# First block's projections taken from x before its norm is known, their products scaled in PSUM; evictions given a higher priority in the recorded order

## The chip, the cores and the metric

The kernel runs on one core of one Trainium2 chip. Its time is the device time of one execution in microseconds (us); lower is better. The kernel before took 1443.79 us, the median of three runs (1440.97, 1443.79, 1444.25). The profile that is read here is of one further execution, which took 1438.14 us; its instructions span 1436.3 us.

## The reference

One layer of a streaming encoder on x of 2048 rows and 1024 columns, float32. The row norm comes first, one input projection feeds three groups of heads, and an output projection with a residual and a second row norm ends it.

```python
hn = rmsnorm(x, norm_g)                       # x * rsqrt(mean(x*x) + EPS) * g
z = jnp.einsum('bsd,de->bse', hn, w_in)       # split into 16 column groups
att = band_chunk_attention(...)               # 6 heads, own 64-row chunk and 8 before it
h_ml = mlstm_chunkwise(...)                   # 6 heads, matrix memory; conv + SiLU on q, k
h_gla = gla_chunkwise(...)                    # 4 heads, per-channel decay from a low-rank gate
y = jnp.concatenate([y_a, y_b, y_c], axis=-1) # each times its own SiLU gate
out = rmsnorm(x + jnp.einsum('bse,ed->bsd', y, w_out), final_g)
```

The row norm multiplies a row of x by one number, and the projection is linear. So the projection of x times g can be taken first and each row's product multiplied by that row's number afterwards: the result is the same up to rounding.

## The kernel before, in words

The rows are cut into four blocks of 512 (`q` = 0 to 3). The projections run block after block; the attention and the output projection follow in a second part, which the change leaves alone.

**One projection.** A projection group fills one PSUM bank `ip` (128 by 512) with 24 matmuls: eight pieces of the contraction, three products each (`x` and `w` are split into a high and a low part in the fp32r format; high by high, high by low, low by high). `proj_g` (L243 to L245) keeps the output columns on the partitions, `proj_t` (L263 to L265) the rows. There are two `ip` banks. TensorE can start the group after next only when both engines that read a bank have read it: that reading is called the eviction (`proj_v`, `silu_tile`, `att_in` and others), done by ScalarE (ACT) and VectorE (DVE). Weights come by DMA into two raw buffers `wraw`, are cast to the high part by ACT (L235) and get their low part from DVE or, for every third one, from GpSimd (POOL) (L236). Five split weights fit at a time.

**The block's norm.** `prep_x` reads the 512 rows of x as they stand (four DMAs), squares and sums them on ACT (L286), takes the power -0.5 on POOL (L288) and puts the 512 numbers on the diagonals of four matrices on DVE (L291). `prep` spreads them over all partitions with one matmul by ones (L298) and a copy (L300), reads the transposed x, `xT`, into four buffers `xraw`, multiplies it by g and the row numbers on DVE (L307) and makes the small gate projection from it (L314). `split_x` makes the high part (ACT, L328) and the low part (DVE or POOL, L329). Only block 0 does this ahead of all projections; blocks 1 to 3 have it done while the block before is projected. `gates` then takes two selections of the gate rows (L336, L343) and runs a chain of logarithms, scans and exponentials on ACT and DVE (L272 to L374).

**The chains.** While a block is projected, three generators put their own matmuls between the projection's: `gla_in` and `gla` (the third head group) and `mlstm` (the second). `gla_in` makes 32 element products per block on POOL (`prd`, L642; `gk`, L639), in groups of four buffers; after each group TensorE sums the four (L648) and so frees the buffers. `gla` needs the blocks `Kt` from POOL (L675) for its matmuls L682.

**What sets the order.** TensorE's order is written by hand: `Flow.piece` adds up the planned time of the projection's matmuls, and a generator's next part is put in when the planned gap after its last part, the second number that it yields, is over. `Flow.need` puts in all that is left of a chain at once. The order on the other engines is made by a scheduler from priorities; `tc.high_priority(offset=AHEAD)` raises the priority of what is issued within it. Each engine runs its own order strictly in turn. At `flow.need("gla_in")`, after the gate projections `proj_gm` of blocks 0, 1 and 2, the rest of `gla_in` is put in with no projection between: this stretch is called the cluster below. After block 3 the chains run out alone: the tail.

## Time and profile before

| | us |
|---|---|
| median of three runs | 1443.79 |
| profiled execution, its own time | 1438.14 |
| its span | 1436.3 |
| TensorE busy in the span | 1325.9 |
| VectorE busy | 791.9 |
| ScalarE busy | 601.7 |
| GpSimd busy | 621.2 |
| first matmul of a block projection | 32.43 |
| last two chains of block 3 run out alone | 981 to 1014 |

The mean granted clock of TensorE was 0.943 of full. A profile line names the line of the kernel, the engine, the operation, and the tiles as output<-inputs; `PE` is TensorE's matmuls, `PEld` its weight loads, `SPq` the queue that issues the DMAs. A wait is put down to the instruction that released it. A busy time of TensorE is not its peak, since matmuls overlap: a group of 24 in a row takes about 5.4 us at the full clock whatever their busy times add up to.

### The profile page before, as it was taken

The page shows a single profiled execution, that of the slowest core. Times are in us where ns is not written, and L with a number is a line of the kernel's source. Part 1 is how long each engine was busy: PE and PEld are TensorE (multiplying, and loading weights), DVE is VectorE, ACT ScalarE, POOL GpSimd, SP SyncE. Part 2 cuts the span into 40 slices and gives each one's busy share as a digit, 9 for nine tenths or more (in the row PEclk, how much of TensorE's full clock was granted, in tenths as well). Part 3 has the DMA queues.
Part 4 walks back from the last instruction along what each step waited for, and adds up shares of the span by engine and source line. Part 5 has one row for each costly group of instructions (what it writes and reads, how often), then busy time and mean ns, then how long its engine had stood idle before and what let it go on. Part 6 is the DMA issues. An engine that isn't in the chain of part 4 may idle for free.

```text
span 1436.3 us, 20063 instructions
## 1 busy us (share of the span) xinstructions
PE 1325.9 (92%) x7044; PEld 1073.8 (75%) x7044; DVE 791.9 (55%) x1886; ACT 601.7 (42%) x1149; POOL 621.2 (43%) x847
## 2 busy tenths in 40 slices
PE   5899989989998998999899899997878999999997
PEld 2688867868886786888678677886766887877876
DVE  7626546762654666264466625646556756656731
ACT  5634312463431246343133524332356555655531
POOL 4215662321665222266533415743246354453442
PEclk7999979999997999999799999998987999999999
DMA  7443214554321455432144533331488464655322
GB/s 248 147 131 100 85 39 123 151 176 128 103 74 39 118 153 178 126 107 73 45 119 126 140 120 104 89 112 49 134 215 257 143 182 128 183 155 156 102 69 87
DMA packets 107206, 180.11 MB, mean 125 GB/s; under 512 B 9824, under 2 KB 54752, under 8 KB 107104
## 3 DMA queue, kind: packets, MB, share of 16 engines
q1 hardware_dynamic: 102496, 170.43, 40.1%
q10 hardware_dynamic: 4608, 8.39, 1.6%
q8 instruction: 56, 0.92, 0.3%
q14 instruction: 46, 0.38, 0.1%
HBM read 143.14 MB, written 35.65 MB: 124 GB/s over the span
## 4 chain that ended last, share of the span: by engine, by line
PE 70%; DVE 10%; DMA 6%; POOL 5%; ACT 4%; issue 4%; SPq 1%; POOLq 0%; DVEq 0%; ACTq 0%
PE ip L243 12%; PE ip L245 12%; PE ip L244 12%; PE s L851 3%; PE ip L975 3%; PE ip L973 3%; PE ip L974 3%; PE ip L263 3%; PE ip L264 3%; PE ip L265 2%; PE tp L915 2%; PE ga L682 2%; DVE pt L865 2%; PE s L554 2%; PE w L932 2%
## 5 line engine op out<-in xcount | busy, mean ns | idle before, releaser
L243 PE MATMUL ip<-x,w 128*128 128x512 f32 x800 | 327.5, 409 | 0.0
L245 PE MATMUL ip<-x,w 128*128 128x512 f32 x800 | 314.0, 393 | 0.0
L244 PE MATMUL ip<-x,w 128*128 128x512 f32 x800 | 314.0, 392 | 0.0
L235 ACT CAST w<-wraw 128x1024 fp32r<-128x1024 f32 x132 | 138.3, 1048 | 264.3 <-PE ip L245 189.9
L236 DVE TENSOR_TENSOR w<-wraw,w 128x1024 fp32r<-128x1024 f32 x88 | 115.3, 1310 | 181.1 <-ACT w L235 180.5
L236 POOL TENSOR_TENSOR w<-wraw,w 128x1024 fp32r<-128x1024 f32 x44 | 106.2, 2413 | 205.6 <-ACT w L235 205.5
L243 PEld LDWEIGHTS ip<-x,w 128*128 128x128 f32 x800 | 151.5, 189 | 43.2 <-issue 13.9
L245 PEld LDWEIGHTS ip<-x,w 128*128 128x128 f32 x800 | 151.3, 189 | 33.2
L244 PEld LDWEIGHTS ip<-x,w 128*128 128x128 f32 x800 | 151.8, 190 | 31.2 <-issue 2.4
L870 POOL TENSOR_SCALAR pt<-pt,sm 128x640 f32<-128x640 f32 (+2 forms) x96 | 70.7, 738 | 150.1 <-DVE sm L869 117.6
L263 PE MATMUL ip<-w,x 128*128 128x512 f32 x256 | 105.2, 411 | 23.1 <-DVE hl L414 21.8
L264 PE MATMUL ip<-w,x 128*128 128x512 f32 x256 | 103.5, 404 | 3.5 <-POOL w L236 2.7
L973 PE MATMUL ip<-wo,y 128*128 128x512 f32 x256 | 106.6, 416 | 0.0
L868 ACT ACTIVATE pt<-pt,sm 128x640 f32<-128x640 f32 (+2 forms) x96 | 73.3, 764 | 71.2 <-DVE sm L865 68.6
L265 PE MATMUL ip<-w,x 128*128 128x512 f32 x256 | 103.0, 402 | 0.0
L975 PE MATMUL ip<-wo,y 128*128 128x512 f32 x256 | 101.2, 395 | 0.3 <-POOL y L881 0.3
L974 PE MATMUL ip<-wo,y 128*128 128x512 f32 x256 | 101.2, 395 | 0.0
L642 POOL TENSOR_TENSOR prd<-gk,zg 128x16 f32<-128x16 f32 (+15 forms) x128 | 75.3, 588 | 59.2 <-PE pw L648 53.0
L921 DVE TENSOR_TENSOR pl<-tp,ph 128x512 fp32r<-128x512 f32 (+2 forms) x126 | 74.6, 599 | 32.4 <-ACT ph L920 31.0
L851 PE MATMUL s<-kk,qq 128*128 128x384 f32 (+1 forms) x360 | 80.9, 335 | 10.2 <-DVE sm L865 8.7
L851 PEld LDWEIGHTS s<-kk,qq 128*128 128x128 f32 x360 | 61.0, 202 | 28.7 <-DVE sm L865 21.9
L263 PEld LDWEIGHTS ip<-w,x 128*128 128x128 f32 x256 | 50.2, 196 | 36.4 <-DVE hl L414 23.5
(244 smaller groups left out, 2447.2 us busy)
## 6 DMA issues: line engine op xcount, KB each, us to landing
wraw<-in_w_f SPq DMA_DIRECT2D x100, 512.0 KB, 3.6
wraw<-in_w_t SPq DMA_DIRECT2D x32, 512.0 KB, 4.0
qq<-q_d SPq DMA_DIRECT2D x48, 256.0 KB, 4.5
kk<-k_d SPq DMA_DIRECT2D x18, 512.0 KB, 6.6
vv<-v_d SPq DMA_DIRECT2D x18, 512.0 KB, 7.5
xraw<-in_x SPq DMA_DIRECT2D x16, 512.0 KB, 5.3
xraw<-in_xT SPq DMA_DIRECT2D x16, 512.0 KB, 7.2
xr<-in_x SPq DMA_DIRECT2D x16, 512.0 KB, 4.0
```

What stands on the lines that cost most here:

```text
L235: nc.scalar.copy(w[:, :, 0, :], rv)
L236: other().tensor_tensor(w[:, :, 1, :], rv, f32(w[:, :, 0, :]), op=ALU.subtract)
L243: nc.tensor.matmul(ps, w[:, k, 0, :], X[k][:, 0, :], start=(k == 0), stop=False)
L244: nc.tensor.matmul(ps, w[:, k, 0, :], X[k][:, 1, :], start=False, stop=False)
L245: nc.tensor.matmul(ps, w[:, k, 1, :], X[k][:, 0, :], start=False, stop=(k == KT - 1))
L263: nc.tensor.matmul(ps, X[k][:, 0, t], w[:, 0, :], start=(k == 0), stop=False)
L264: nc.tensor.matmul(ps, X[k][:, 0, t], w[:, 1, :], start=False, stop=False)
L265: nc.tensor.matmul(ps, X[k][:, 1, t], w[:, 0, :], start=False, stop=(k == KT - 1))
L851: nc.tensor.matmul(sp[:, :cn], qq[:, l, tt * P:(tt + 1) * P], kk[:, ko + c0:ko + c0 + cn], start=(l == 0), stop=(l == 1))
L973: nc.tensor.matmul(ps, Y[k][:, 0, t], wo[k, j][:, 0, :], start=(e == 0), stop=False)
L974: nc.tensor.matmul(ps, Y[k][:, 0, t], wo[k, j][:, 1, :], start=False, stop=False)
L975: nc.tensor.matmul(ps, Y[k][:, 1, t], wo[k, j][:, 0, :], start=False, stop=(e == KT - 1))
```

## The change

Five things are changed.

- **Block 0 starts from raw x.** The rows of x are not read for block 0; `xT` is, at once after the first weight and the vector g. `first_x` makes the high part of x times g on ACT (L277), the low part on DVE (L278), and eight tiles of squares of x, four on ACT and four on POOL. `first_z` projects `gq`; after each of the eight pieces four float32 matmuls (L293) add that piece's squares over the partitions, by a column of ones, into the bank `ss`. From this come the row numbers `rs`, the diagonals `dg`, and, after the group `gk`, the spread numbers `rbs`. `gq` and `gk` are multiplied by them as they are evicted; the gate projection uses weights times g and is multiplied as well.
- **All later products of block 0** are multiplied in their bank before their eviction: DVE L338 in `proj_t` (8 times), DVE L263 in `proj_f` (24 times).
- **Evictions** in `proj_t`, `silu_tile`, `proj_z`, `proj_m` and `att_in` are issued within `tc.high_priority(offset=AHEAD)`.
- **Two planned gaps are shorter:** 6.0 in place of 7.0 before each summing of `gla_in`, 0.5 in place of 4.0 after each chunk of `gla`.
- Calls are moved so that this holds; the other blocks' norms are made as before.

```diff
         def proj_f(name, X):
...
+            if "rbs" in lead:
+                scale_f(out_[0])
             return out_[0]
+        def scale_f(ps):
+            with tc.high_priority(offset=AHEAD):
+                nc.vector.tensor_tensor(ps, ps, lead["rbs"], op=ALU.mult)
+        def first_x():
+            raws, X, sq = [], [], []
+            with tc.high_priority(offset=2 * AHEAD):
+                nc.sync.dma_start(ng, norm_g)
+                w0 = load_w(w_f[_F.index("gq")], KT)
+                for g in range(4):
...
+                    nc.sync.dma_start(raw, xT[:, 2 * g:2 * g + 2, 0:QT])
+            for k in range(KT):
+                src = raws[k // 2][:, k % 2, :]
+                xk = xs.tile([P, 2, QT], FR, name="x")
+                nc.scalar.activation(xk[:, 0, :], src, AF.Copy, scale=ng[:, k:k + 1])
+                nc.vector.scalar_tensor_tensor(xk[:, 1, :], src, ng[:, k:k + 1], f32(xk[:, 0, :]), op0=ALU.mult, op1=ALU.subtract)
+                sq.append(g_tile([P, QT]))
+                if k % 2 == 0:
+                    nc.scalar.activation(sq[k], src, AF.Square)
+                else:
+                    nc.gpsimd.tensor_tensor(sq[k], src, src, op=ALU.mult)
...
+        def first_z(R):
+            raws, X, sq, w0 = first_x()
+            ss = bank("pw")
+            for k, _ in enumerate(proj_g("gq", X, out_, 1, w0)):
+                for tt in range(NC):
+                    nc.tensor.matmul(ss[:, tt:tt + 1], sq[k][:, tt * P:(tt + 1) * P], ones[:, 0:1],
...
+            nc.gpsimd.tensor_tensor(rs, rs, mhalf[:, 0:NC], op=ALU.pow)
...
+            for _ in proj_g("gk", X, out_, KT):
+                pass
+            rb = bank("pw")
+            nc.tensor.matmul(rb, ones, dg.rearrange("p a t -> p (a t)"), start=True, stop=True)
...
+            nc.scalar.copy(rbs, rb)
...
+                nc.vector.scalar_tensor_tensor(z[:, 0, :], out_[0], 32.0 ** -0.5, rbs, op0=ALU.mult, op1=ALU.mult)
+                nc.vector.tensor_tensor(z[:, 1, :], out_[1], rbs, op=ALU.mult)
...
-                evac(tt, ps)
+                with tc.high_priority(offset=AHEAD):
+                    if "rs" in lead:
+                        nc.vector.tensor_scalar(ps, ps, lead["rs"][:, tt:tt + 1], None, op0=ALU.mult)
+                    evac(tt, ps)
...
-                        yield 0.0, 7.0
+                        yield 0.0, 6.0
...
-                    yield 0.25, 4.0
+                    yield 0.25, 0.5
...
-        flow.start("prep", prep(0, R, prep_x(0)))
         load_consts()
-        flow.finish("prep")
-        X = split_x(R["raws"])
+        X, z0 = first_z(R)
```

Three places of the new order matter for what follows. Lines after the change are higher by about 70: L272 becomes L343, L414 becomes L487, L642 becomes L721, L675 becomes L754.

**ScalarE at the start.** Before, with `g<-pw` the copy of the spread row numbers:

```order
L286 ACTIVATE xraw,rs<-xraw 128x1024 x3
L235 CAST w<-wraw 128x2x512 x2
L300 COPY g<-pw 128x512
L328 CAST x<-xraw 128x512 x6
L235 CAST w<-wraw 128x2x512
```

Now, with `dd<-pw` that copy:

```order
L277 ACTIVATE x<-xraw,ng 128x512 x3
L281 ACTIVATE g<-xraw 128x512
L235 CAST w<-wraw 128x8x128
L235 CAST w<-wraw 128x2x512 x4
L308 COPY dd<-pw 128x512
L235 CAST w<-wraw 128x2x512
```

The copy stood behind two casts of the value weights (`128x2x512`) and now stands behind four.

**VectorE in the gate chain of block 1.** `hl<-ip` is the eviction of the first value group's banks; the first bank is free after the second of these. Before:

```order
L356 TENSOR_TENSOR g<-g 6x512
L629 TENSOR_TENSOR qt<-zg,qt 128x256
L633 TENSOR_TENSOR Dt<-Dt,dl 128x2
L414 TENSOR_TENSOR hl<-ip,hl 128x3x64
L629 TENSOR_TENSOR qt<-zg,qt 128x256
L633 TENSOR_TENSOR Dt<-Dt,dl 128x2
L628 TENSOR_TENSOR lc<-lc,zg 128x256 x2
L359 TENSOR_TENSOR g<-g 6x512
L633 TENSOR_TENSOR Dt<-Dt,dl 128x2x2 x2
L414 TENSOR_TENSOR hl<-ip,hl 128x3x64
L361 TENSOR_TENSOR g<-g 6x512
```

Now:

```order
L432 TENSOR_TENSOR g<-g 6x512
L436 TENSOR_TENSOR rows<-g,ml 6x128
L437 TENSOR_TENSOR rows<-g 6x384
L712 TENSOR_TENSOR Dt<-Dt,dl 128x2x2
L434 TENSOR_TENSOR hl_nm<-g,hl_nm 6x512
L712 TENSOR_TENSOR Dt<-Dt,dl 128x2x2
L487 TENSOR_TENSOR hl<-ip,hl 128x3x64
L712 TENSOR_TENSOR Dt<-Dt,dl 128x2x3 x2
L445 TENSOR_TENSOR hl_iw<-rows,hl_iw 6x4
L712 TENSOR_TENSOR Dt<-Dt,dl 128x2x4 x2
L712 TENSOR_TENSOR Dt<-Dt,dl 128x2x5
L487 TENSOR_TENSOR hl<-ip,hl 128x3x64
```

L432, L436, L437 and L434 are the old L361, L365, L366 and L363: they stood behind the two evictions and now stand ahead of them.

**TensorE in block 0's cluster.** Before, the cluster's first rows, from the first sum of the second half (`32x256 x4`) on, with no projection between:

```order
L648 MATMUL pw<-prd,hs_157 32x256 x4
L600 MATMUL mt<-ident,m 128x128 x3
L521 MATMUL s<-hl_nm,sel 128x128 x6
L729 MATMUL gb<-ident,n 128x128 x2
L648 MATMUL pw<-prd,hs_157 32x16x5
L648 MATMUL pw<-prd,hs_157 32x16x6
L648 MATMUL pw<-prd,hs_157 32x16x7
L648 MATMUL pw<-prd,hs_157 32x16x8
L531 MATMUL s<-qk 128x128 x6
L535 MATMUL mt<-ident,qk 128x128 x3
L678 MATMUL gb<-ident,dr 128x128
L679 MATMUL gb<-ident,kd 128x128
```

Now its first rows are:

```order
L727 MATMUL pw<-prd,hs_157 32x16x7
L727 MATMUL pw<-prd,hs_157 32x16x8
L679 MATMUL mt<-ident,m 128x128 x3
L600 MATMUL s<-hl_nm,sel 128x128 x6
L808 MATMUL gb<-ident,n 128x128 x2
L757 MATMUL gb<-ident,dr 128x128
L758 MATMUL gb<-ident,kd 128x128
L761 MATMUL ga<-Qb,Kt 128x64 x7
L727 MATMUL pw<-prd,hs_157 32x16x9
L727 MATMUL pw<-prd,hs_157 32x16x10
L727 MATMUL pw<-prd,hs_157 32x16x11
L727 MATMUL pw<-prd,hs_157 32x16x12
```

The first of the four sums (`32x256 x4`) left the cluster: it stands 36 projection matmuls earlier. The `mlstm` matmuls that stood behind the old L682 (L549, L554, L566) left it too, to behind the next half group of the projection. On POOL the seven `Kt` of this chunk (L754) stand behind the products of the third group of four; on TensorE their user L761 stands ahead of that group's sums.

More of the change, by code (lines that the diff above doesn't have):

```diff
@@ L237, in load_w, with proj_g @@
             return w
-        def proj_g(name, X, out_, per):
-            w = load_w(w_f[_F.index(name)], KT)
+        def proj_g(name, X, out_, per, w=None):
+            w = load_w(w_f[_F.index(name)], KT) if w is None else w
             ps = bank("ip", 2)
@@ L394, in sig_tile @@
             th = ev.tile([P, QT], FP32, name="e")
-            nc.scalar.activation(th, ps, AF.Tanh, scale=0.5)
+            with tc.high_priority(offset=AHEAD):
+                nc.scalar.activation(th, ps, AF.Tanh, scale=0.5)
             return th
@@ L430, in proj_z @@
             z = big.tile([P, 2, QT], FP32, name="zg", bufs=1)
-            nc.scalar.activation(z[:, 0, :], proj_f("gq", X), AF.Copy, scale=32.0 ** -0.5)
-            nc.scalar.copy(z[:, 1, :], proj_f("gk", X))
+            pq = proj_f("gq", X)
+            with tc.high_priority(offset=AHEAD):
+                nc.scalar.activation(z[:, 0, :], pq, AF.Copy, scale=32.0 ** -0.5)
+            pk = proj_f("gk", X)
+            with tc.high_priority(offset=AHEAD):
+                nc.scalar.copy(z[:, 1, :], pk)
             return z
@@ L448, in proj_m @@
                 zb = big.tile([P, 3 + QT], FP32, name="u", bufs=1)
-                nc.scalar.copy(zb[:, 3:], ps)
+                with tc.high_priority(offset=AHEAD):
+                    nc.scalar.copy(zb[:, 3:], ps)
                 if st["zb"] is None:
@@ L481, in att_in @@
             scl = 0.125 if b < 3 else 1.0
-            nc.scalar.activation(hl[:, 0, :], ps, AF.Copy, scale=scl)
-            nc.vector.scalar_tensor_tensor(hl[:, 1, :], ps, scl, f32(hl[:, 0, :]), op0=ALU.mult, op1=ALU.subtract)
+            with tc.high_priority(offset=AHEAD):
+                nc.scalar.activation(hl[:, 0, :], ps, AF.Copy, scale=scl)
+                nc.vector.scalar_tensor_tensor(hl[:, 1, :], ps, scl, f32(hl[:, 0, :]), op0=ALU.mult, op1=ALU.subtract)
             if b < 3:
@@ L757, in trunk_kernel @@
             qk = proj_m(X)
+            if lead:
+                rbs = big.tile([P, 3 + QT], FP32, name="u", bufs=1)[:, 0:QT]
+                nc.vector.tensor_copy(rbs, lead["rbs"])
+                lead["rbs"] = rbs
             M = dict(R)
@@ L765, in trunk_kernel @@
             proj_a(q, X)
+            lead.clear()
             if q + 1 < NQ:
```

33 lines of the change are left out of this document (30 added, 3 removed).

## The prediction

> **What bounds the kernel now.** I read the page's engine rows and its chain first, then TensorE's waits up to 1090 us (the projections and the hand-over to the attention; the change leaves the rest alone), then single stretches.
>
> ```profile
> PE 1325.9 (92%) x7044; PEld 1073.8 (75%) x7044; DVE 791.9 (55%) x1886; ACT 601.7 (42%) x1149; POOL 621.2 (43%) x847
> PE 70%; DVE 10%; DMA 6%; POOL 5%; ACT 4%; issue 4%; SPq 1%; POOLq 0%; DVEq 0%; ACTq 0%
> ```
>
> TensorE is the bound in most stages, so only its stalls and its slow-clock stretches can be won. Its waits name where they are (releaser: us, times, longest):
>
> ```profile
> PE ip L263 <- DVE hl L414: 21.8, 4, 6.4
> PE pw L648 <- POOL prd L642: 14.8, 12, 2.6
> PE mt L600 <- DVE m L591: 11.5, 3, 5.9
> PE pw L298 <- DVE g L291: 9.1, 1, 9.1
> PE pw L314 <- DVE xraw L307: 6.9, 2, 5.1
> ```
>
> The first is one stall in each of the four blocks, at the third bank of the values; the second is the clusters; the third the tail; the last two the start. The stretches themselves (length; busy PE, PEld, DVE, ACT, POOL; granted clock; DMA share; GB/s):
>
> ```profile
> 0.00:32.40 32.40, 15.32 (x46) 7.87 (x46) 23.14 (x53) 17.88 (x25) 16.99 (x27) 0.74 0.75 251
> 184.90:209.70 24.80, 19.05 (x123) 14.65 (x122) 12.76 (x38) 4.75 (x10) 18.04 (x37) 0.64 0.12 36
> 305.80:311.00 5.20, 0.35 (x2) 0.00 (x0) 5.00 (x18) 3.46 (x9) 0.70 (x3) 1.00 0.17 68
> 311.00:314.50 3.50, 3.46 (x8) 2.79 (x9) 3.36 (x12) 2.45 (x7) 0.89 (x3) 0.52 0.41 115
> 435.10:461.60 26.50, 19.85 (x124) 15.32 (x123) 11.41 (x37) 4.74 (x10) 19.47 (x38) 0.67 0.12 32
> 686.40:711.40 25.00, 19.25 (x123) 14.66 (x122) 12.76 (x38) 4.75 (x10) 18.22 (x37) 0.64 0.12 35
> 981.10:1014.30 33.20, 21.65 (x171) 19.34 (x171) 20.48 (x67) 6.19 (x14) 8.19 (x19) 0.79 0.18 45
> ```
>
> Row by row: the start, block 0's cluster, block 1's value stall and the 3.5 us after it, the clusters of blocks 1 and 2, the tail. After the stall TensorE was granted 0.52 of its clock, in the clusters about 0.65: a stall costs more than its own length.
>
> **Term 1, the start and block 0.** Ahead of the first projection stood the norm of block 0.
>
> ```profile
> 6.85 3.90 DVE L236 TENSOR_TENSOR w<-wraw,w 128x1024 fp32r<-128x1024 f32 x1 [0.74 <-ACT w L235]
> 7.34 2.33 POOL L236 TENSOR_TENSOR w<-wraw,w 128x1024 fp32r<-128x1024 f32 x1
> 28.98 2.41 DVE L307 SCALAR_TENSOR_TENSOR xraw<-xraw,ng,g 128x512 f32<-128x512 f32 x2
> 29.13 3.95 SPq L285 DMA_DIRECT2D xraw<-in_x  x3
> 32.43 0.50 PE L243 MATMUL ip<-x,w 128*128 128x512 f32 x1
> 41.13 1.06 ACT L286 ACTIVATE xraw<-xraw 128x1024 f32<-128x1024 f32 x1 [1.25 <-DMA xraw<-in_x]
> 43.61 0.59 ACT L272 ACTIVATE g<-pw 128x512 f32<-128x512 f32 x1
> 45.24 0.39 PE L263 MATMUL ip<-w,x 128*128 128x512 f32 x1
> 55.71 0.97 DVE L291 TENSOR_SCALAR g<-ident,rs 128x128 f32<-128x128 f32 x4
> 63.50 0.78 DVE L363 TENSOR_TENSOR hl_nm<-g,hl_nm 6x512 fp32r<-6x512 f32 x1
> 69.08 0.39 PE L263 MATMUL ip<-w,x 128*128 128x512 f32 x1
> 74.88 0.48 PE L263 MATMUL ip<-w,x 128*128 128x512 f32 x1
> L154 PE MATMUL pw<-ones 128*128 128x128 f32 x28 | 6.3, 427 | 1.1 <-DVE ones L122 1.1
> L329 DVE TENSOR_TENSOR x<-xraw,x 128x512 fp32r<-128x512 f32 x4 | 2.6, 679 | 0.0
> L329 POOL TENSOR_TENSOR x<-xraw,x 128x512 fp32r<-128x512 f32 x2 | 3.3, 1658 | 3.9 <-ACT x L328 3.9
> L235 ACT CAST w<-wraw 128x1024 fp32r<-128x1024 f32 x5 | 5.2, 1043 | 7.0 <-DMA wraw<-in_w_t 4.3 <-DMA wraw<-in_w_f 2.7
> ```
>
> Now `gq` can start when one piece of x is split. The eight low parts on DVE take 0.68 (L329) to 1.2 us each (L307, 2.41 for two): 5.4 to 9.6, behind the first weight's split, which took until 10.75. The 32 sums of squares are float32 products of two passes each; the nearest row is the warm-up L154, 28 passes in 6.3, 0.22 us each, so 64 take up to 14 us and half of that at twice the clock. With 5.4 for the 24 main products (48 and two selections filled 32.43 to 45.24) that is 13 to 19.5 us from about 9 on: `gq` ends between 22 and 28, I take 24, nearer to the full clock since TensorE is then dense. `gk` adds 5.4, the spreading matmul (two passes of 512 columns, some 0.9 by the 0.22 for 128) and its copy (0.6, like L272) 1.5, the first scaled eviction about 1: the values start at 32. The copy L308 stands behind four weight casts, each behind a DMA (L235: 7.0 us idle, most on DMA), which allows up to 35; the least is 28. So TensorE is 13 us ahead of 45.24 (10 to 17).
>
> The Trainium skill (SBUF — State Buffer, "Who interferes with whom") says a VectorE instruction with two SBUF inputs and a GpSimd one that reads SBUF exclude each other for a whole instruction. The 3.90 us of DVE beside POOL's 2.33 agree. By it the four POOL squares (1.66 each, like L329 on POOL) can hold the low parts up by 6.6 us, and the values would start 2 to 3 us later than by the sum.
>
> But the gate chain does not come 13 us earlier. It waits on ACT and DVE for the squares of the next block's rows, whose loads need the `xraw` buffers that the gate projection reads last, at about 33. Before, from the issue at 29.13 to the last square's end was 13.1 us, so that end is about 45; from L272 to the end of L291 (43.61 to 56.68) were 13.1 more, and in the new order the second bank's second `hl` stands behind L362, the old L291: with 0.7 for both `hl`, the second bank is free at 59 and the fourth value group starts then, against 69.08. The first bank's next eviction stands behind the rest of the chain (56.68 to 64.28, 7.6 us), a weight split (1.2), two scalings (L273's 0.69 each below) and two `hl`: 11 more, 70. The second value part then starts at 70 against 74.88: **5 us won** of the 13. Bounds: 9 if only TensorE's own work counts (59 + 5.4 + 1.7 of slow clock = 66), 1 if start and loads take their late ends.
>
> **Term 2, the scalings of block 0.** 32 more DVE instructions; the nearest row, same shape from PSUM:
>
> ```profile
> L273 DVE TENSOR_SCALAR ls<-pw 128x512 f32<-128x512 f32 x4 | 2.8, 692 | 1.6 <-ACT g L272 1.5
> ```
>
> 0.7 us each on an engine 55% busy, and a bank has 5.4 us while the other fills: covered by TensorE's own group. Without cover 32 x 0.7 = 22; I take 0.5 lost, 0 to 3.
>
> **Term 3, the value stall of blocks 1 to 3.** What decides is when the second `hl` of the first bank is done:
>
> ```profile
> 302.58 1.23 DVE L236 TENSOR_TENSOR w<-wraw,w 128x1024 fp32r<-128x1024 f32 x1
> 310.63 0.35 DVE L414 TENSOR_TENSOR hl<-ip,hl 128x192 fp32r<-128x192 f32 x1
> 311.01 0.69 DVE L361 TENSOR_TENSOR g<-g 6x512 f32<-6x512 f32 x1
> 312.68 0.78 DVE L363 TENSOR_TENSOR hl_nm<-g,hl_nm 6x512 fp32r<-6x512 f32 x1
> ```
>
> In blocks 1 and 2 the new order puts L361 to L363 (311.01 to 313.46, 2.4 us) ahead of it: despite the higher priority the eviction is later, and TensorE, queued behind the bank, with it. On ACT the chain's first step now has a weight cast (1.05) and an eviction of `zg` (0.6, the shape of L272's 0.59) ahead of it that L272 had not: 1.6. The split L236 leaves the chain in block 1 (-1.2). So +2.8 in block 1 and +4.0 in block 2 (each 0 to 5); block 3 had these steps ahead already: 0 (-1.5 to 1.5). **7 us lost.**
>
> **Term 4, the clusters.** Within 184.90 to 209.70, POOL's groups; behind them one of the moved groups of matmuls, 20 us earlier:
>
> ```profile
> L642 POOL TENSOR_TENSOR prd<-gk,zg 128x80 f32<-128x80 f32 (+11 forms) x12 | 6.9, 576 | 6.8 <-PE pw L648 6.3
> L639 POOL TENSOR_TENSOR gk<-gk,al 128x80 f32<-128x80 f32 (+10 forms) x11 | 5.7, 515 | 0.6
> L675 POOL TENSOR_TENSOR Kt<-lc,Dt 128x16 f32<-128x16 f32 (+6 forms) x7 | 1.9, 291 | 0.0
> L471 POOL TENSOR_TENSOR gm<-e 128x512 f32<-128x512 f32 x1 | 1.3, 1256 | 0.0
> 163.23 1.55 PE L554 MATMUL s<-v,dd 128*128 128x65 f32 x12
> ```
>
> POOL idled 6.3 us for buffers that TensorE freed late. The first sum now comes three half groups earlier, so the second four products are made during the projection; eight instructions of (6.9 + 5.7) / 23 = 0.55 make four, 4.4. What is left in turn on POOL: third four (4.4), `gm` (1.3), `Kt` (1.9), fourth four (4.4): 12, behind 2 us of waiting for the second. TensorE waits some 6 us for `Kt`, since L761 stands ahead of the third sums, and the rest then runs at about half clock. POOL sets the length: 2 + 12, then TensorE's last sums and what overlaps badly, 18 in all. The matmuls L549, L554 and L566 come back behind it, about 2.8 (L554's 12 passes took 1.55, the other 18 are narrower or fewer). 24.8 - 18 - 2.8 = **4 us** each, 12 for three, between 0 (POOL held by a weight split as well) and 18. Where the stall goes: from POOL's products to `Kt`.
>
> The Trainium skill (TensorE: Matmul & The Clock Gate, "HAM oscillation — how this bites in real kernels") wants no idle gap of TensorE over about 3.4 us. Here that speaks against the change: the single 6 us wait is over it, where the old short waits were under it. The old cluster had 0.64 all the same; if only the long wait cost the clock, the new cluster would win 2 us rather than 4.
>
> **Term 5, the tail.** Two chunks of `mlstm` still follow each other after the last projection, 33.2 us as before; `ga` matmuls now stand ahead of `mlstm` ones: 1 lost (-1 to 4).
>
> **Sum:** -5 + 0.5 + 7 - 12 + 1 = -8.5. Against the profiled execution, 1438.14 with a span of 1436.3 and 1.8 around it, that is 1429.6; the median of the three runs is 5.65 higher, 1443.79, and the same step from it gives **1435**.
>
> **Rivals.**
> - *The start is kept whole* (20%): if the loads of the next rows do not hold the gate chain, 13 of the 13 us stay, and with clusters at 6 each: -13 + 0.5 + 7 - 18 + 1 = -22.5, 1421. For it: four tiles of 512 KB no longer cross the DMA at the start, 8 us at the 251 GB/s of the first row. Against it: the row 41.13, a square that waited for its load.
> - *No change* (20%): the clusters win nothing, because POOL's own 18 busy us of 24.8 set their length. -5 + 0.5 + 7 + 1 = +3.5: 1447. Against it: the 6.3 us that POOL idled.
> - *The evictions come later everywhere* (15%, slower): a bank waits for a DVE queue in which the gate chain stands first; each of blocks 1 to 3 loses 6 us, block 0 wins 1: -1 + 18 - 12 + 1.5 = +6.5, 1450. It decides from 4 us a block on, where it has used up the 11.5 that the other terms leave. This is the change not doing what it says; the order already shows it in blocks 1 and 2.
> - The forecast, 45%, has 1429 to 1441 as its own range.
>
> About 0.3%, 4.3 us, can be told from no change. The forecast is faster by that in 8 of 10 of its share (0.36), the first rival wholly (0.20), "no change" now and then (0.03): faster 0.59. Same: 0.08 of the forecast, 0.13 of "no change", 0.04 of the third: 0.25. Slower: 0.01, 0.04 and 0.11: 0.16. The range 1420 to 1449 leaves out the ends of the first and third rival.
>
> **What would show it.** Term 1: the first value matmul at 28 to 35 us, the fourth group at 59, the second part at 70. Term 3: the wait for `hl` at 8 us in blocks 1 and 2, and L434 ahead of it on DVE. Term 4: the wait for `prd` shrinks, a new one on `Kt` of about 6 us in L761 appears, each cluster under 22 us. Wrong if the value stall shrinks below 4 us in blocks 1 to 3, or the clusters keep 24 us.

## The result, and the profile after

The changed kernel took 1426.47 us, the median of five runs (1425.04 to 1430.07); the kernel before took 1442.87 beside it (five runs, 1435.60 to 1444.25). The ratio is 0.9902, 95% interval 0.9873 to 0.9932: 10 to 18 us faster. The profiled execution took 1429.36 us with a span of 1427.6, against 1438.14 and 1436.3: 8.7 us less span. The kernel before spreads over some 10 us from run to run (in later sets its median was 1438.9 to 1440.7), so what follows compares inside one set of runs where it can, or stretch by stretch in the traces. The changed kernel was timed in the first set alone: a difference between medians of two sets is good to some 4 us only.

The page's engine row of the changed kernel:

```profile
PE 1330.0 (93%) x7108; PEld 1080.2 (76%) x7108; DVE 812.6 (57%) x1916; ACT 598.7 (42%) x1143; POOL 614.8 (43%) x849
```

Of its TensorE waits up to 1080 us, those that bear on the terms (releaser: us, times, longest):

```profile
PE ip L331 <- DVE hl L487: 23.1, 5, 6.3
PE mt L679 <- DVE m L670: 12.5, 4, 5.1
PE gb L757 <- DVE n L810: 8.2, 4, 3.0
PE pw L727 <- POOL prd L721: 4.8, 4, 1.8
```

The two long waits of the old start are gone and the wait for `prd` fell from 14.8 to 4.8 us. The wait for `hl` is as long as before but comes five times, not four, and a wait for `n` is new. Next, stretches as in the prediction (length; busy PE, PEld, DVE, ACT, POOL; granted clock; DMA share; GB/s). Of the kernel before, the values and gate groups of block 0, and what lies between its cluster and block 1's values:

```profile
45.24:109.41 64.17, 57.81 (x252) 47.15 (x250) 28.62 (x67) 28.22 (x53) 15.69 (x24) 0.95 0.37 109
210.03:294.34 84.31, 84.29 (x472) 68.07 (x472) 52.32 (x110) 31.56 (x54) 22.04 (x28) 0.99 0.48 145
```

Of the changed kernel, the start, the same two stretches with the cluster between them, the other two clusters, and the tail:

```profile
0.00:43.95 43.95, 39.40 (x158) 33.16 (x158) 19.27 (x54) 17.75 (x23) 20.19 (x31) 0.69 0.43 138
43.95:114.99 71.04, 62.49 (x258) 49.98 (x255) 37.32 (x81) 33.67 (x63) 17.71 (x24) 0.93 0.46 151
191.03:205.57 14.54, 11.45 (x86) 8.64 (x84) 9.79 (x26) 4.20 (x9) 12.35 (x24) 0.77 0.19 61
205.57:299.74 94.17, 88.15 (x502) 70.98 (x502) 60.86 (x135) 36.51 (x59) 26.77 (x34) 0.98 0.48 146
442.32:458.95 16.63, 11.93 (x86) 8.82 (x84) 9.96 (x26) 4.20 (x9) 13.46 (x25) 0.79 0.21 58
690.29:706.85 16.56, 13.04 (x87) 9.07 (x85) 9.21 (x23) 4.21 (x9) 13.63 (x25) 0.65 0.19 53
971.93:1005.85 33.92, 23.27 (x166) 20.96 (x164) 21.09 (x67) 5.70 (x13) 8.12 (x19) 0.75 0.14 36
```

Block 0's values lost 6.9 us, more than the 1.3 that the start won; the clusters are 9 to 11 us shorter, and the stretch behind the first is 10 us longer. All these kernels hold the same 132 projection groups in the same order, so each trace can be cut where a group's first matmul starts, and the cuts compared. The table does so, in us of one profiled execution each. "Values" runs from a block's first value matmul to the end of its two gate groups, "cluster" from the last projection matmul ahead of it to the first behind it, "behind" from there to the next block's first value matmul. The stretches between values and clusters are left out: they differ by under 1.2 us.

| stretch | before | changed | start_only | gaps_only | gap6_only | gap05_only | no_start | wide_r | gates_early | fold |
|---|---|---|---|---|---|---|---|---|---|---|
| start | 45.2 | 44.0 | 44.0 | 44.8 | 45.2 | 45.1 | 44.4 | 29.4 | 29.3 | 29.4 |
| values 0 | 64.2 | 71.0 | 69.3 | 64.5 | 64.2 | 64.6 | 64.2 | 70.6 | 68.1 | 65.8 |
| cluster 0 | 25.5 | 14.5 | 25.5 | 15.0 | 14.3 | 28.5 | 14.3 | 15.0 | 14.7 | 15.1 |
| behind 0 | 84.3 | 94.2 | 85.2 | 90.6 | 103.4 | 85.4 | 89.1 | 96.3 | 93.8 | 96.3 |
| values 1 | 64.2 | 65.4 | 66.7 | 60.3 | 58.0 | 65.9 | 62.7 | 63.1 | 64.0 | 62.7 |
| cluster 1 | 26.8 | 16.6 | 25.5 | 16.3 | 16.3 | 26.7 | 16.4 | 14.6 | 14.3 | 18.3 |
| behind 1 | 84.7 | 89.9 | 84.5 | 87.9 | 98.4 | 87.0 | 87.4 | 91.3 | 90.8 | 90.9 |
| values 2 | 63.5 | 64.2 | 63.9 | 63.1 | 61.5 | 63.4 | 63.4 | 59.6 | 62.4 | 63.2 |
| cluster 2 | 25.5 | 16.6 | 26.7 | 14.9 | 15.5 | 25.4 | 14.4 | 16.8 | 15.6 | 16.5 |
| behind 2 | 84.1 | 87.1 | 84.9 | 92.4 | 102.2 | 85.3 | 91.7 | 87.3 | 86.2 | 86.2 |
| values 3 | 69.6 | 62.4 | 63.0 | 62.5 | 61.2 | 68.1 | 63.3 | 61.8 | 61.6 | 61.5 |
| tail | 33.4 | 33.9 | 36.2 | 34.9 | 34.4 | 35.5 | 33.5 | 34.3 | 34.5 | 33.8 |
| after the tail | 422.0 | 421.8 | 423.9 | 421.0 | 425.0 | 418.6 | 423.2 | 420.7 | 418.6 | 418.7 |

From before to changed: the start and block 0's values +5.6; the clusters -30.0; what stands behind them +18.1; the values of blocks 1 and 2 +2.0, of block 3 -7.2; the stretches that are left out +2.5; the tail +0.5; after it -0.2. That is the 8.7 us.

### The profile page after: what moved, and what is told of

The parts are those of the page before. It is cut to its first block, busy times and chain, and to the rows that moved or that the text cites. A ratio compares the mean times of both kernels' runs of the same rounds, so it can differ in the third digit from the quotient of the medians.

```text
span 1427.6 us, 20212 instructions
## 1 busy us (share of the span) xinstructions
PE 1330.0 (93%) x7108; PEld 1080.2 (76%) x7108; DVE 812.6 (57%) x1916; ACT 598.7 (42%) x1143; POOL 614.8 (43%) x849
## 4 chain that ended last, share of the span: by engine, by line
PE 71%; DVE 12%; DMA 5%; ACT 5%; issue 3%; POOL 3%; SPq 0%; POOLq 0%; DVEq 0%; ACTq 0%
PE ip L243 13%; PE ip L245 12%; PE ip L244 12%; PE s L932 3%; PE ip L1056 3%; PE ip L331 3%; PE ip L1055 2%; PE ip L332 2%; PE ip L1054 2%; PE ip L333 2%; DVE pt L946 2%; PE tp L996 2%; DMA wraw<-in_w_o 2%; PE w L1013 2%; PE ga L761 2%
## 5 line engine op out<-in xcount | busy, mean ns | idle before, releaser
L243 PE MATMUL ip<-x,w 128*128 128x512 f32 x800 | 332.0, 415 | 1.7 <-ACT x L277 1.7
L244 PE MATMUL ip<-x,w 128*128 128x512 f32 x800 | 316.4, 395 | 1.0 <-DVE x L278 1.0
L245 PE MATMUL ip<-x,w 128*128 128x512 f32 x800 | 316.9, 396 | 0.0
L333 PE MATMUL ip<-w,x 128*128 128x512 f32 x256 | 103.4, 404 | 0.0
L721 POOL TENSOR_TENSOR prd<-gk,zg 128x16 f32<-128x16 f32 (+15 forms) x128 | 76.4, 597 | 30.8 <-PE pw L727 23.9
L932 PEld LDWEIGHTS s<-kk,qq 128*128 128x128 f32 x360 | 58.9, 196 | 31.5 <-DVE sm L946 25.9
```

The costliest lines, as they stand in the source:

```text
L243: nc.tensor.matmul(ps, w[:, k, 0, :], X[k][:, 0, :], start=(k == 0), stop=False)
L244: nc.tensor.matmul(ps, w[:, k, 0, :], X[k][:, 1, :], start=False, stop=False)
L245: nc.tensor.matmul(ps, w[:, k, 1, :], X[k][:, 0, :], start=False, stop=(k == KT - 1))
L333: nc.tensor.matmul(ps, X[k][:, 1, t], w[:, 0, :], start=False, stop=(k == KT - 1))
L932: nc.tensor.matmul(sp[:, :cn], qq[:, l, tt * P:(tt + 1) * P], kk[:, ko + c0:ko + c0 + cn], start=(l == 0), stop=(l == 1))
```

## The experiments

### One part at a time

**start_only** is the changed kernel with both gaps put back (7.0 and 4.0) and the evictions outside `tc.high_priority`.

```diff
-                        yield 0.0, 6.0
+                        yield 0.0, 7.0
...
-                    yield 0.25, 0.5
+                    yield 0.25, 4.0
```

> The kernel before with only block 0's start on raw x and the scalings of block 0; the evictions keep their old priority, the planned gaps are 7.0 and 4.0. Theory A, read from the two traces group by group: the start loses time, since TensorE ran the sums of squares at half clock until 36.4 us and the value part of block 0 then stalled twice; from the first matmul of the program to the end of block 0's values it cost 5.6 us. So about 1448 to 1449 (+5 to +6), with the first value matmul at 44 us and half clock from 9 to 36 us again. Rival, the sum on record: the start wins 4.5 us, about 1438.

1444.54 us against 1438.9: ratio 1.0042 (1.0027 to 1.0056). The start alone makes the kernel slower, by 6 us, as theory A had it, but not all at the place that it named: in this trace the start and block 0's values cost 3.9 us of the 5.4 that the span grew, and the rest is a balance of later stretches (among them block 1's values +2.5, the tail +2.8, block 3's values -6.6). The changed kernel's own trace shows where the start loses; start_only has its first value matmul at the same 44.0 us and the same half clock. The sums of squares on TensorE, from 8.3 to 33.5 us (count, busy us, mean ns), and the stretch at the half clock:

```profile
L293 PE MATMUL pw<-ones,g 128*128 128x1 f32 x64 | 13.6, 334 | 0.0
```

```profile
9.10:36.40 27.30, 26.58 (x94) 23.73 (x95) 10.81 (x17) 11.30 (x16) 8.82 (x8) 0.50 0.34 106
```

The sums took 13.6 us, just inside the estimate of up to 14. But the products between them took twice their time too (one started every 0.43 us, against 0.23 at the full clock): TensorE was busy for 26.58 of 27.30 us and was granted half its clock throughout. So the first value matmul came at 43.95. The second matter is the gate chain's second selection, in the timeline of TensorE (start, duration), before and after:

```profile
41.65 1.02 PE L343 MATMUL pw<-g,gsel 128*128 128x512 f32 x2
```

```profile
53.16 1.02 PE L414 MATMUL pw<-g,gsel 128*128 128x512 f32 x2
```

It stood inside the second group, ahead of the values, and now stands one and a half banks into them: the chain's work on VectorE comes 11.5 us later and falls on the banks behind. Rows of VectorE's and GpSimd's timelines there, in order of time:

```profile
62.40 1.31 DVE L419 TENSOR_TENSOR_SCAN g<-g,zero 6x512 f32<-6x512 f32 x1
63.64 1.50 DVE L423 TENSOR_TENSOR_SCAN g<-ones,g 6x128 f32<-6x128 f32 x4
65.17 0.95 DVE L362 TENSOR_SCALAR g<-ident,rs 128x128 f32<-128x128 f32 x4
66.04 0.34 DVE L487 TENSOR_TENSOR hl<-ip,hl 128x192 fp32r<-128x192 f32 x1
...
72.58 2.36 POOL L236 TENSOR_TENSOR w<-wraw,w 128x1024 fp32r<-128x1024 f32 x1
72.81 2.68 DVE L432 TENSOR_TENSOR g<-g 6x512 f32<-6x512 f32 x1
76.36 0.75 DVE L338 TENSOR_SCALAR ip<-ip,rs 128x512 f32<-128x512 f32 x1
77.86 0.36 DVE L487 TENSOR_TENSOR hl<-ip,hl 128x192 fp32r<-128x192 f32 x1
```

TensorE stood still twice, until 66.44 and until 78.27 us, right behind the two `hl` shown (8.6 us of waiting; before, one wait of 5.6). Ahead of the first stand the scans and the diagonals. Ahead of the second stand a step of the chain that took 2.68 us beside a weight split on GpSimd, and the new multiplication.

**gaps_only** is the kernel before with only the two gaps changed, 7.0 to 6.0 and 4.0 to 0.5.

> The kernel before with only the two planned gaps shortened (6.0 for 7.0, 0.5 for 4.0). Theory A, from the two traces: each cluster is 8 to 10 us shorter, but the groups behind it take back 10, 4 and 3.5 us, because the chain's matmuls and their waits moved there; net 0, -6 and -5, together about -11, so 1432. The value stalls of blocks 1 to 3 stay as before, 5 to 6.6 us. Rival, the sum on record: -4 for each cluster, nothing given back behind it, +1 in the tail, also -11: the two differ in the segments, not in the time.

1415.91 us against 1438.9: ratio 0.9842 (0.9823 to 0.9862), 23 us faster, twice what both expectations gave. The clusters are 31.5 us shorter in all, 17.8 come back behind them as expected, and then the values of blocks 1 and 3 are 3.9 and 7.1 us shorter, which neither had. This part alone beats the whole change.

**prio_only** is the kernel before with only the evictions at the higher priority, in `proj_t` as shown and likewise in `silu_tile`, `proj_z`, `proj_m` and `att_in`.

```diff
-                evac(tt, ps)
+                with tc.high_priority(offset=AHEAD):
+                    evac(tt, ps)
```

> The kernel before with only the evictions at the higher priority. Theory A: block 3's value part is 7.7 us shorter (stall 3.3 for 6.6, no wait for the weight split, no half clock behind it), blocks 1 and 2 are 0.8 and 2.9 us longer, together about -4, so 1439. Rival, the sum on record: blocks 1 and 2 lose 2.8 and 4.0 and block 3 nothing, +7, so 1450. Second rival: block 3's gain came from the shorter gaps, which moved other work away from VectorE there; then block 3 keeps its 6.6 us stall here and the time is 1443 to 1447.

1438.84 us against 1438.9: ratio 0.9993 (0.9976 to 1.0010). Nothing is gained or lost, and block 3's values keep their length (69.5 us). The sum on record and theory A both fall. The second rival has this right, that the priority is not what shortened block 3, but not its 1443 to 1447, and the gaps are not the only thing that shortens it (below).

**no_start** is the changed kernel with the old start; gaps and priorities are kept.

> The changed kernel without its start: the norm of block 0 ahead of the projections as before, no scalings; priority and shorter gaps are kept. Theory A: the start's loss of 5.6 us is taken back, so 5 to 6 us below the changed kernel, about 1421. Rival, the sum on record: the start's gain of 4.5 is lost, so about 1431.

1417.03 us: ratio 0.9848 (0.9829 to 0.9867). It is as fast as gaps_only, so the priority does nothing beside the gaps either, and 9 us faster than the changed kernel, which theory A put at 5 to 6. By the traces 6.4 us lie in the start and block 0's values, 5.1 in what stands behind cluster 0 and 2.7 in the values of block 1; behind 2 loses 4.6 again.

### Which gap

**gap6_only** is the kernel before with 6.0 for 7.0 alone, **gap05_only** with 0.5 for 4.0 alone.

> The kernel before with only the gap ahead of each summing of the third head group's products cut from 7.0 to 6.0. Both gaps together gave 1415.9, 23 us below the kernel before. Theory: it is this gap that takes four of the sixteen sums and the end of an mlstm chunk out of each cluster, so the clusters are 9 to 11 us shorter here too, and most of the gain is here: 18 to 22 us, 1417 to 1421. Rival: half of the gain comes from the other gap, which brings the chunks of the third head group forward behind the cluster; then 8 to 12 us here, 1427 to 1431.

> The kernel before with only the gap after each chunk of the third head group cut from 4.0 to 0.5. Theory: the clusters keep all sixteen sums and their 24 to 26 us; 0 to 4 us are won behind them, 1435 to 1439. Rival: half of the gain is here, 8 to 12 us, 1427 to 1431.

gap6_only took 1444.55 us against 1439.66: ratio 1.0045 (1.0029 to 1.0062), slower. gap05_only took 1441.86: 1.0014 (0.9992 to 1.0037), no change that can be told. Neither theory held: each gap alone wins nothing, both together 23 us. TensorE's waits behind block 0's cluster, from 198 to 305 us, with 6.0 alone:

```profile
PE mt L600 <- DVE m L591: 4.4, 1, 4.4
PE pw L343 <- ACT g L340: 4.2, 1, 4.2
PE gb L729 <- DVE n L724: 1.3, 1, 1.3
```

and with both gaps, in gaps_only:

```profile
PE ip L263 <- DVE hl L414: 2.6, 1, 2.6
PE mt L600 <- DVE m L591: 1.9, 1, 1.9
```

With the 6.0 four of the sixteen sums leave the cluster, and the end of its last chunks moves to the projections behind. With the old 4.0 the next chunk of `gla` (L729) is then put in at the same half group as a step of `mlstm` (L600), and a later one between the two gate selections (L336, L343): TensorE has steps of two chains back to back, with no projection between them to cover the other engines' answers, and waits 4.4 and 4.2 us. The stretch took 103.4 us in place of 84.3. The three waits are 9.9 of these 19.1 us; the rest is busy time of TensorE, which has 49 matmuls more there. The values of block 1 get 6 back. With 0.5 the chunks of `gla` come half a group earlier, one wait of 1.9 is left there, and the stretch takes 90.6. The 0.5 alone leaves all sixteen sums in the cluster (28.5 us).

### The sums and the clock

**wide** is the changed kernel with the squares as the moving and the ones as the stationary operand. **wide_r** has the squares and the ones in the fp32r format besides.

```diff
-                for tt in range(NC):
-                    nc.tensor.matmul(ss[:, tt:tt + 1], sq[k][:, tt * P:(tt + 1) * P], ones[:, 0:1],
-                                     start=(k == 0 and tt == 0), stop=(k == KT - 1 and tt == NC - 1), skip_group_check=True)
+                nc.tensor.matmul(ss, ones, sq[k], start=(k == 0), stop=(k == KT - 1))
...
+                nc.vector.tensor_tensor(di, ss.rearrange("p (a t) -> p a t", a=NC), ident.unsqueeze(1).broadcast_to([P, NC, P]), op=ALU.mult)
+                nc.vector.tensor_reduce(out=rs, in_=di, axis=mybir.AxisListType.X, op=ALU.add)
```

> The changed kernel, with the sums of squares made the other way round: the ones are the stationary operand and each tile of squares (512 columns) the moving one, in float32; 8 products in place of 32, and three VectorE instructions pick the row numbers out. Theory A: the 64 passes of one column with a weight load each do not count as activity for the clock, which stayed at half from 9 to 36 us; with 512 columns a pass TensorE is granted its full clock by 13 to 17 us, and although the sums are more work (16 us at half clock, 8 at full, against 13.6 at half), the second projection group ends at 30 to 34 us, not 40.3, and the value part starts at 33 to 37, not 44. Time 2 to 7 us below the changed kernel, if the value stalls do not take it back. Rival B: the clock stays at half for another reason (the two short waits at 6.4 to 9.8 us, or the start itself) until some 36 us; then the sums take 16 us in place of 13.6, the value part starts at 45 to 47, and the time is 0 to 4 us above the changed kernel.

> As the run before it in this list, with squares and ones in the fp32r format, so that each sum is one pass of 512 columns (8 x 0.23 us at full clock, 0.43 at half). By both theories the sums cost 2 to 4 us in place of 13.6. Theory A: first projection group done at 18 to 20 us, the second at 24 to 26, the value part starts at 27 to 31 us. Rival B, half clock until 36 us whatever TensorE does: 22 to 24, 33 to 35 and 36 to 38 us. What the time makes of it depends on the stalls of block 0's value part, which the first theory puts down to the gate chain falling on the same stretch: if they stay (4.3 and 4.6 us), 6 to 14 us below the changed kernel.

wide took 1419.27 us, ratio 0.9868 (0.9848 to 0.9889); wide_r 1406.63, 0.9778 (0.9758 to 0.9798). Two stretches of wide, from its first products to the end of its second group:

```profile
8.80:16.10 7.30, 6.59 (x11) 3.66 (x12) 6.72 (x9) 7.24 (x12) 3.36 (x4) 0.53 0.85 265
16.10:31.90 15.80, 15.20 (x55) 10.08 (x54) 8.16 (x14) 4.81 (x6) 6.69 (x4) 1.00 0.38 117
```

The clock is full from 16.1 us on, as theory A had it: with 512 columns a pass, and the ones as weights, it opens, although TensorE is no busier than in the changed kernel and the format is the same. The first value matmul came at 35.7 us (33 to 37 expected), in wide_r at 29.4 (27 to 31). The values of block 0 stayed long, 72.5 and 70.6 us, and the gain of the start arrived all the same: 8.3 and 14.6 us of it, and spans that are 10.7 and 20.8 us shorter than the changed kernel's. wide's median is 7.2 us below it (2 to 7 expected), wide_r's 19.8 (6 to 14 expected). The rest of wide_r's gain is in stretches that were not edited (values 2, cluster 1, values 1).

### The stalls of block 0's values

**squares_late** and **gates_early** stand on wide_r: the first makes the squares in `prep_x` wait for the gate chain through their scale, the second also cuts a gap in `gates`.

```diff
+            if q == 1:
+                sc = one.tile([P, 1], FP32, name="after_gates")
+                nc.vector.tensor_scalar(sc, rows[:, 0:1], 1.0, 1.0, op0=ALU.max, op1=ALU.min)
...
-                nc.scalar.activation(xt, xt, AF.Square, accum_out=rs[:, tt:tt + 1])
+                nc.scalar.activation(xt, xt, AF.Square, scale=sc, accum_out=rs[:, tt:tt + 1])
```

```diff
-            yield 0.9, 3.0
+            yield 0.9, 3.0 if q else 0.0
```

> The changed kernel with the sums in fp32r by 512 columns (1406.6 us, first value matmul at 29.4, block 0's value and gate part from there 70.6 us against 64.2 before), and in addition the squares of block 1's rows made to wait for the gate chain of block 0, so that they can not stand ahead of it on ScalarE. Theory on record: the gate chain is held by these squares and their loads, so it comes 4 to 8 us earlier, and the value part shrinks to 63 to 67 us; 1399 to 1403. Rival, from the traces: the chain is held by its second selection, which stands on TensorE one bank into the values (38.6 us; before, at 41.7, it stood ahead of them); nothing moves, two stalls of 4 to 5 us stay, 70 to 71 us, 1405 to 1408.

> As squares_late, and the second selection of block 0's gate rows is put in one half group earlier (its planned gap 0 in place of 3.0): some 35.5 in place of 38.6 us. Theory: the chain's place against the value banks sets the stalls; 3 us earlier, its VectorE work falls on the second bank and the wait behind the third, so the two stalls become one of 4 to 6 us or two shorter ones, the value part 65 to 68 us, 1400 to 1404. Rival: wherever the chain falls, its VectorE work (scans, weight splits) stands ahead of two evictions; stalls of 8 to 10 us in sum stay, 70 to 71 us and 1405 to 1408.

squares_late took 1411.93 us, ratio 0.9805 (0.9781 to 0.9829); gates_early 1400.73, 0.9736 (0.9713 to 0.9759). The chain's first step on the second selection, in ScalarE's timeline of wide_r, squares_late and gates_early:

```profile
40.84 0.61 ACT L346 ACTIVATE g<-pw 128x512 f32<-128x512 f32 x1
```

```profile
39.40 0.60 ACT L346 ACTIVATE g<-pw 128x512 f32<-128x512 f32 x1 [1.56 <-PE pw L421]
```

```profile
37.92 0.60 ACT L346 ACTIVATE g<-pw 128x512 f32<-128x512 f32 x1 [0.56 <-PE pw L421]
```

and TensorE's wait for `hl` from 25 to 100 us in wide_r and in gates_early:

```profile
PE ip L334 <- DVE hl L490: 8.4, 2, 4.7
```

```profile
PE ip L334 <- DVE hl L494: 5.8, 1, 5.8
```

Without the squares ahead of it the chain came 1.4 us earlier and then waited for the selection (`pw L421`): the squares held it by that much at most, not by the 4 to 8 us of the theory on record. With the selection earlier as well there is one stall in place of two, and the values take 68.1 us, at the edge of the 65 to 68 of the theory. The time of squares_late is not told from wide_r's (their intervals overlap); a stretch elsewhere that took longer is shown below.

**no_scale** is wide_r without the 32 multiplications: it leaves this part of the computation out, to price it. **fold** is gates_early with eight of them made by the evictions of the values (`s` is the row number, and 1.0 in blocks 1 to 3).

```diff
-                    nc.scalar.copy(v5[:, :, b, b, :], pv4[:, :, b, :])
-                    nc.vector.tensor_tensor(v5[:, :, b, 1 - b, :], pv4[:, :, b, :], f32(v5[:, :, b, b, :]), op=ALU.subtract)
+                    nc.scalar.activation(v5[:, :, b, b, :], pv4[:, :, b, :], AF.Copy, scale=s)
+                    nc.vector.scalar_tensor_tensor(v5[:, :, b, 1 - b, :], pv4[:, :, b, :], s, f32(v5[:, :, b, b, :]), op0=ALU.mult, op1=ALU.subtract)
```

> The changed kernel with the sums in fp32r by 512 columns, without the 32 multiplications of block 0's products by the row numbers (only gq, gk and the gate rows are still scaled): this part of the computation is left out, which prices it. Sum on record: 0.5 us, 0 to 3, so 1404 to 1406.6. Rival: the multiplications stand in the queue of VectorE between a full bank and its eviction, at both stalls; 0.75 us and a hand-over each time, 5 to 8 us in the value part alone, 1399 to 1402.

> As gates_early (1400.7 us; one stall of 6.0, value part 68.05), with the eight multiplications of block 0's value products folded into their evictions: the copies on ScalarE take the row number as their scale, the subtraction on VectorE becomes a multiply and subtract. The 24 multiplications of the later groups stay. Theory, from the run without any multiplication (value part 3.8 us shorter): most of their price is in the value part, so 64 to 66 us there and 1396 to 1399. Rival: the one stall that is left is set by the scans and the diagonals that stand ahead of the eviction, not by the multiplication; value part 67 to 68.5 us, 1399 to 1402.

no_scale took 1401.71 us, ratio 0.9744 (0.9722 to 0.9766). Its block 0 values took 66.8 us in place of 70.6, which prices the multiplications at 3.8 us there. What they cost beyond that can't be told: the medians, of two sets, differ by 4.9, and other stretches of the two traces move as much either way (behind cluster 0 -3.4, values 2 +3.8). fold brought the values from 68.1 to 65.8, as expected, and was not faster all the same: 1405.91, ratio 0.9772 (0.9747 to 0.9796), an interval that overlaps that of gates_early. The largest loss is in cluster 1, which the edit does not touch. The cluster of fold, and in it GpSimd's timeline:

```profile
422.52:440.85 18.33, 13.28 (x86) 8.59 (x84) 9.84 (x26) 4.21 (x9) 13.46 (x25) 0.67 0.18 51
```

```profile
436.32 0.23 POOL L719 MEMSET Dt<- 128x162 f32 x1 [2.23 <-DVE Sst L800]
436.51 0.88 POOL L730 TENSOR_TENSOR prd<-gk,zg 128x240 f32<-128x240 f32 x1
```

The same in gates_early:

```profile
422.90:437.17 14.27, 11.49 (x87) 8.12 (x85) 9.02 (x25) 4.20 (x9) 12.25 (x24) 0.76 0.24 65
```

```profile
434.44 0.71 POOL L728 TENSOR_TENSOR prd<-gk,zg 128x240 f32<-128x240 f32 x1
435.92 0.64 POOL L728 TENSOR_TENSOR prd<-gk,zg 128x256 f32<-128x256 f32 x1
436.50 0.23 POOL L717 MEMSET Dt<- 128x162 f32 x1
```

In fold the scheduler put the clearing of `Dt` ahead of the last two products. It waited 2.23 us for VectorE, the products behind it, TensorE behind those, and the cluster ran at 0.67 of the clock. squares_late has the same order there and also took 18.4 us for this cluster. Another 2.5 us of fold are lost behind cluster 0, and their cause stays open. gates_early is the fastest kernel found that computes the whole layer, 2.6% below the kernel before.

## Why the prediction was right, and where it was not

The forecast was 1435 and faster; the runs gave 1426.5, faster, inside the range of 1420 to 1449 but below the forecast's own 1429 to 1441. For the profiled execution it was 1429.6, and 1429.36 was measured. That agreement is chance: two terms were off by 10 and 12 us, in opposite directions.

**Term 1, the start (-5; with term 2, -4.5; measured +5.6).** Wrong in sign. The step that failed first is "nearer to the full clock since TensorE is then dense": dense it was, and the clock stayed at half until 36.4 us. wide shows that the passes of one column, each with a weight load of its own, were the reason; which of the two counts, no run separates. So the first value matmul came at 43.95, not at 28 to 35. The second failed step is that the gate chain waits for the squares of the next block's rows: that is worth 1.4 us in squares_late; what held the chain was its second selection, which the change itself moved one and a half banks into the values; moved 1.6 us forward in gates_early, it brought the chain 1.5 us forward. The prediction's own figures also give 46, not 45, for the end of those squares (33 and 13.1). The fourth value group started at 66.4 (59 forecast), the second value part at 78.3 (70).

**Term 2, the scalings (+0.5).** Too small: 3.8 us by no_scale in block 0's values alone, beyond its bound of 3. "Covered by TensorE's own group" fails where VectorE's queue is the wait, since each multiplication there stands between a full bank and its eviction.

**Term 3, the value stall (+7; measured -5.2).** Wrong in sign. The stall was expected at 8 us in blocks 1 and 2. The longest wait for `hl` was 6.3 in block 1 (4.9 before), 5.1 in block 2 (4.9) and 3.2 in block 3 (6.4), and the values changed by +1.3, +0.7 and -7.2 us. The order that was read is there, L434 ahead of L487, but the term took the rest of the chain to stand still or come later. In block 2 the first scan of the gate rows, in VectorE's timeline before and after:

```profile
553.24 1.28 DVE L348 TENSOR_TENSOR_SCAN g<-g,ml 6x512 f32<-6x512 f32 x1
```

```profile
552.52 1.28 DVE L419 TENSOR_TENSOR_SCAN g<-g,ml 6x512 f32<-6x512 f32 x1
```

The block's first value matmul is at 546.31 and at 548.89 us, so the scan begins 6.9 us behind it before and 3.6 after: the chain comes 3.3 us earlier, and that pays for the steps that stand ahead of the eviction. For block 3 the term had 0 "since it had these steps ahead already". There one of the scans ran beside a weight split on GpSimd before, and alone after:

```profile
799.07 3.43 DVE L621 TENSOR_TENSOR_SCAN lc<-rst,ls 128x256 f32<-128x256 f32 x2
799.40 2.55 POOL L236 TENSOR_TENSOR w<-wraw,w 128x1024 fp32r<-128x1024 f32 x1 [15.07 <-ACT w L235]
```

```profile
794.89 1.27 DVE L700 TENSOR_TENSOR_SCAN lc<-rst,ls 128x256 f32<-128x256 f32 x2
```

Every third low part is dealt to GpSimd in turn, and the new start has eight fewer of them, so in all later blocks it is another split that goes there; the prediction did not look at this. start_only shows what it is worth. Its gaps and its priority are the old ones and its first scan begins 3.4 us behind the first value matmul, as before, but the split on GpSimd is over at 801.55 us:

```profile
807.31 1.27 DVE L692 TENSOR_TENSOR_SCAN lc<-rst,ls 128x256 f32<-128x256 f32 x2
```

Its block 3 values take 63.0 us in place of 69.6. The gaps are a second way to the same gain. gaps_only deals as before, and has a scan beside a split in block 3 too (its VectorE and GpSimd there):

```profile
782.48 1.28 DVE L348 TENSOR_TENSOR_SCAN g<-g,ml 6x512 f32<-6x512 f32 x1
783.69 3.69 DVE L352 TENSOR_TENSOR_SCAN g<-ones,g 6x128 f32<-6x128 f32 x4
783.92 2.39 POOL L236 TENSOR_TENSOR w<-wraw,w 128x1024 fp32r<-128x1024 f32 x1 [12.10 <-ACT w L235]
```

Its values take 62.5 us all the same: the first scan of the gate rows begins 2.3 us behind the first value matmul (780.23), before 6.9. Its chain is forward, and so is the second selection that the chain follows: in block 3 it begins 6.4 us ahead of the first value matmul, against 3.6 in the kernel before and in start_only. In every trace with the 6.0 it begins 6.3 us or more ahead in blocks 1 to 3, in every one with the 7.0 at most 4.5. So the 6.0 brought the chain forward in the changed kernel too. In block 3 the other deal comes on top, and either alone is enough there.

**Term 4, the clusters (-12).** Right in size, by another way: -30.0 in the clusters, +18.1 behind them and 2.5 ahead, -9.4 in all. The wait for `prd` shrank and the clusters are under 22 us, as said. POOL's turn did set the length, as the term has it. Its first and last products in cluster 0, with `Kt` and the user of `Kt` on TensorE between them:

```profile
191.84 0.47 POOL L721 TENSOR_TENSOR prd<-gk,zg 128x144 f32<-128x144 f32 x1 [2.17 <-PE pw L727]
196.44 2.73 PE L761 MATMUL ga<-Qb,Kt 128*128 128x64 f32 x14
198.52 1.83 POOL L754 TENSOR_TENSOR Kt<-lc,Dt 128x16 f32<-128x16 f32 x7
204.33 0.64 POOL L721 TENSOR_TENSOR prd<-gk,zg 128x256 f32<-128x256 f32 x1
```

The turn took 13.1 us here and 15.2 and 14.2 in the other two clusters, for 12 forecast. What failed is the rest of the 18: the 2 us ahead of it were 0.8, and the 4 behind it, for the last sums and what overlaps badly, were 0.6, 0.6 and 1.6. The wait for `Kt` failed too. The seven `Kt` stand in that turn, but L761 begins before them: they belong to the next chunk. The new wait is the one for `n`, 3.0 us at the longest. And "2.8 us come back" was 9.9, 5.2 and 3.0. That the 6.0 alone is slower, and wins only with the 0.5, was in no step: the term costed the cluster by the 6.0, and the 0.5 was left to the tail.

**Term 5, the tail (+1).** It measured +0.5.

Of the rivals, the kept start did not come about in the change; wide_r comes near it, 9.4 us ahead of the kernel before at the end of block 0's values. "The evictions come later everywhere" falls with prio_only, where no block's values moved by more than 0.9 us. "No change" had the clusters win nothing, and they won. Of the two conditions for being wrong, the stall under 4 us was met in block 3 alone, and the clusters of 24 us nowhere.

## What to carry to other kernels

A product with one moving column and a weight load for each pass kept TensorE busy but not at its full clock: put the data on the moving side, which brought the first value matmul from 44.0 to 35.7 us here in the same format. Where planned gaps set the order of several chains, try them together and look where the work that left a stall comes back; one gap alone was slower and both won 23 us. Compare a forecast with the trace term by term: here its sum for the profiled execution was right within 0.3 us while two of its five terms had the wrong sign.

## What the runs showed of the hardware

- TensorE, busy for 26.58 of 27.30 us, was granted 0.50 of its clock throughout, until 3 us behind the last pass of one column; with 512 columns a pass the clock was full 7.3 us after the first products. The Trainium skill (TensorE: Matmul & The Clock Gate, "What's actually happening") has the full clock after one busy window of about 3.4 us. Here eight times that did not do, so the measurement decides: what counts there is not the busy time that a profile shows.
- A pair of VectorE scans took 3.43 us beside a GpSimd weight split and 1.27 alone. The Trainium skill (SBUF — State Buffer, "Who interferes with whom") says that a VectorE instruction with two SBUF inputs and a GpSimd one that reads SBUF exclude each other; these rows agree. The 2 us lie on the path of a bank: without the split beside the scans, block 3's values took 63.0 us in place of 69.6 in start_only.
